# A two-block network in one launch: parked S5 matrices loaded pair by pair, small mixer weights split early, low parts of weights placed by clocks that know DVE and POOL exclude each other

## The chip, the cores and the metric

One core of a Trainium2 chip runs the whole program in one launch. The metric is the device time of one execution in microseconds; the kernel before takes 3071.73 us (median of three runs: 3071.64, 3071.73, 3073.94).

## The reference

Two blocks, one behind the other, on 256 tokens of 1024 numbers, all in float32. The first is a mixer of four kinds (differential attention, block attention, gated linear attention, a gated recurrence) and a mixture of 32 experts. The second has two layers, and each layer is three residual steps. The lines that matter here:

```python
for i in range(DEPTH_2):                                   # two layers
    f = swiglu(rmsnorm(h, ffn1_pre_g[i]), ...)             # 1024 -> 2 x 2816 -> 1024
    h = h + 0.5 * rmsnorm(f, ffn1_post_g[i])
    m = mixer(rmsnorm(h, mix_pre_g[i]), ...)
    h = h + rmsnorm(m, mix_post_g[i])
    f = swiglu(rmsnorm(h, ffn2_pre_g[i]), ...)
    h = h + 0.5 * rmsnorm(f, ffn2_post_g[i])
# the mixer of block 2
z, xbc, dt_raw, u5, g_a, g_b = split(u @ w_in)
y_a = ssd_branch(z, xbc, dt_raw, ...) @ w_branch_a         # state space, 4 groups of 8 heads, chunks of 128
y_b = s5_branch(u5, lam, b, c, ..., w_glu) @ w_branch_b    # complex diagonal recurrence, 64 groups
return (sigmoid(g_a) * y_a + sigmoid(g_b) * y_b) @ w_out
```

The S5 branch is computed in blocks of four tokens with matrices made from its parameters alone (powers of the eigenvalues times the input matrix, a Toeplitz matrix, an output matrix G, an array of powers E).

## The kernel before

**Weights.** A weight unit is 1 MB, a raw tile of 128 x 2048 float32, loaded by one DMA on SP into one of three raw buffers (`NRAW`). It has two halves of 128 x 1024. For each half ACT casts a high part (`whi`) and `tensor_sub` makes the low part (`wlo`, raw minus high) on DVE or on POOL; there are four pairs of high and low buffers. A half then feeds 24 matmuls of 128 x 256: three products (high x high, high x low, low x high) for each of eight slices. All of block 2's weights go this way: the two feed-forward steps of a layer (`ffn`), and in the mixer the stages u (input of S5), z, x and g (mixed in one plan, with the SSD's chunks between them), `glu` and `bb` (end of the S5 branch), `ba` (end of the SSD branch) and `wo`.

**What sets the order.** The order on every engine is fixed when the program is built, by a planner. `Clocks` and `Engine` keep an estimated clock for each engine (line 155 is the helper through which every instruction of block 2 and most of block 1 is issued; so the profile's lines are nearly all L155, and the work is told apart by the tiles' names). Side work is written as generators (threads): a thread issues a few instructions and yields; `yield n` with a whole number waits for ticks, with a float for that many microseconds of the planner's TensorE clock. `stir` steps, between groups of matmuls, those threads whose inputs would be ready by the clocks. `low(h)` chooses the engine of a low part: POOL, if POOL would be done in time for its matmuls or sooner than DVE, else DVE. `static` is the mode of the mixture of experts, whose order is written out by hand.

**Parked matrices.** Block 1 makes the S5 matrices while TensorE is waiting for expert weights and parks them in DRAM (`ld`, `kd`, `gd`, `ed`). `s5_build` is a thread that fetches them, in ffn1 of layer 0 and, for layer 1, in ffn2 of layer 0: for each half of the groups four loads of `ld` and four of the input matrix `s5_bt` (each 64 x 1024, 256 KB), eight small ones of `kd`, then a complex product (`cmul`, 12 instructions of 128 x 1024 on both halves), and last four loads of E and four of G (512 KB each). All go through SP's queue, where the weights are loaded too.

**Mixer.** `mixer` loads at its start the convolution's weights (`cw`) and the 1024 x 32 weight of dt (`dtw`), and scales and splits them in `small_weights` behind the third u unit; `ssd_steps` computes dt and its running sums from 32 rows (chain `dt`), transposes them on TensorE and hands over to four `ssd_group` threads, one for each group of heads. All four must have finished before `ba`.

Of the kernel before, what the change touches and what calls it, by code (L numbers as in the profile page):

```python
# [15 lines left out]
P = 128  # L16
# [26 lines left out]
class Clocks:  # L43
# [4 lines left out]
    def __init__(self, nc):  # L48
        self.nc, self.times, self.base = nc, {}, {}
        self.dma = self.queue = self.end = 0.0  # L50
        self.count, self.table = 0, None
        self.vector, self.gpsimd = Engine(nc.vector, self.on_vector, self), Engine(nc.gpsimd, self.on_gpsimd, self)
        self.scalar, self.tensor, self.sync = Engine(nc.scalar, self.on_scalar, self), Engine(nc.tensor, self.on_tensor, self), Engine(nc.sync, None, self)
# [52 lines left out]
    def busy(self, name):  # L106
        return max([max(t[:2]) for t in self.times.get(name, {}).values()], default=0.0)

    def on_vector(self, name, out, args, kw):
        n = max(a.free_size() for a in (out, *args) if isinstance(a, bass.AP))  # L110
        return 0.07 + 0.06 * any(isinstance(a, bass.AP) and a.free_size() == 1 for a in args) + n * (0.0063 if name == "reciprocal" else 0.00052 if name in self.SINGLE else 0.00104)
# [19 lines left out]
class Engine:  # L131
# [3 lines left out]
    def __getattr__(self, name):  # L135
        f, c = getattr(self.engine, name), self.clocks

        def call(out, *args, **kw):
            w = [out] + [kw[k] for k in ("accum_out",) if k in kw]
            r = [a for a in (*args, *kw.values()) if isinstance(a, bass.AP) and a is not kw.get("accum_out")]  # L140
            start = max([self.clock] + [c.written(a, self) for a in r] + [c.touched(a, self) for a in w])
            if name == "dma_start":
                self.clock = start + (1.0 if self is c.gpsimd else 0.1)
                c.queue = max(c.queue, start) + 0.45
                c.dma = max(c.dma, c.queue + 1.1) + self.spread(out, r)
                end = c.dma + 1.9
            else:
                end = self.clock = start + self.cost(name, out, args, kw)
            for a in w:
                c.mark(a, end, self)  # L150
            for a in r:
                c.mark(a, end)
            c.end = max(c.end, end)
            c.count += 1
            return f(out, *args, **kw)  # L155
        return call
# [22 lines left out]
class Core:  # L179
# [6 lines left out]
    NRAW = 3  # L186
    GAP = 20.0, 10.0, 25.0, 12.0
    LENT = ()
# [170 lines left out]
    def low(self, h):  # L359
# [4 lines left out]
        hi = c.written(self.halves[h][0])  # L364
        pool = max(self.q.clock, hi) + 2.3
        return self.q if pool <= max(c.tensor.clock + (h - self.uh) * 2.57 - self.LEAN, max(self.v.clock, hi) + 1.14) else self.v

# [74 lines left out]
    def step(self, th):  # L442
# [6 lines left out]
        if isinstance(th.wait, float):  # L449
            th.ready = c.tensor.clock + th.wait  # L450
        if th.done:
# [148 lines left out]
class Block2(Core):  # L600
# [406 lines left out]
    def s5_build(self, l, res):  # L1007
# [5 lines left out]
        self.lab = "s5b"  # L1013
        toep, win = [], []
        for hf in range(2):
            yield self.GAP[hf]
            yield from self.need(p4=8)
            self.lab = "s5b"
            tp = self.p4([P, H, 64])
            LT = self.p4([P, H, 64]), self.p4([P, H, 64])  # L1020
            BT = self.p4([P, H, 64]), self.p4([P, H, 64])
            for g in range(2):
                rows = slice(g * 64, g * 64 + 64)
                for ri in range(2):
                    nc.sync.dma_start(LT[ri][rows], dram_ap(ld, ((ri * 2 + g) * 4 * NP + hf * H) * 64, [[NP * 64, 4], [0, 16], [1, H * 64]]))
                    nc.sync.dma_start(BT[ri][rows], dram_ap(a["s5_bt"], (((l * 2 + ri) * 2 + g) * 16 * NP + hf * H) * 64,
                                                            [[0, 4], [NP * 64, 16], [1, H * 64]]))
                for j in range(4):
                    r0 = g * 64 + j * 16
                    nc.sync.dma_start(tp[r0:r0 + 16], dram_ap(kd, hf * H * 32 * 112 + g * 16 * 112 + (3 - j) * 16,  # L1030
                                                              [[112, 16], [32 * 112, H], [1, 64]]))
# [5 lines left out]
            self.give(p4=3 if hf else 5)  # L1037
            toep.append(tp)
            win.append((wr, wi))
        yield from self.need(p4=8)  # L1040
        self.lab = "s5b"
        G = [[self.p4([P, H, 4, 16]) for _ in range(2)] for _ in range(2)]
        E = [[self.p4([P, H, 64]) for _ in range(2)] for _ in range(2)]
        for hf in range(2):
            for ri in range(2):
                half = slice(ri * 1024, ri * 1024 + 1024)
                nc.sync.dma_start(E[hf][ri].rearrange("p h m -> p (h m)"), made["ed"][hf, :, half])
                nc.sync.dma_start(G[hf][ri].rearrange("p h k c -> p (h k c)"), made["gd"][hf, :, half])
            yield self.GAP[3]
        res.update(win=win, toep=toep, G=G, E=E, r4=made["r4"])  # L1050
# [143 lines left out]

    def ssd_steps(self, l, dps, r, res):

        nc, a, v = self.nc, self.a, self.v
        self.lab = "dt"
        hvt = self.t([32, 2], "hvt")
        nc.gpsimd.dma_start(hvt, a["hvec"][l])  # L1200
        y, e, u, w_, dt, adt, ac = (self.p1()[:32] for _ in range(7))
# [21 lines left out]
        for c in range(2):  # L1223
            cc = slice(c * P, c * P + P)
            v.tensor_tensor_scan(ac[:, cc], self.one32, adt[:, cc], 0.0, op0=ALU.mult, op1=ALU.add)
        yield 2
        yield from self.need(ps=1)
# [152 lines left out]


    def mixer(self, l, h, banks, build, s5):
        nc, a = self.nc, self.a
# [3 lines left out]
        self.lab = "u5"  # L1387
        cw = self.t([P, 24, 5], "cw")
        nc.sync.dma_start(cw, a["conv2"][l])
        dtw = self.p1([P, KD, 32])  # L1390
        nc.sync.dma_start(dtw, a["wdt"][l])
        dw = self.p1([P, KD, 32], F32R), self.p1([P, KD, 32], F32R)
        ud = self.scratch([1024, T], "ud")
# [37 lines left out]

        def small_weights():
            v.tensor_scalar_mul(cw, cw, 0.5)
            nc.scalar.copy(dw[0], dtw)
            yield
            v.tensor_sub(dw[1], dtw, dw[0].bitcast(F32))
# [14 lines left out]
        sd = {}  # L1451
        self.spawn(self.ssd_steps(l, dps, r, sd))
        self.finish(sc)
# [153 lines left out]
    def block2(self, h, layers=2, first=None):  # L1607
# [1389 lines left out]
```

## Time and profile before

| | us |
|---|---|
| median of three runs | 3071.73 |
| the profiled execution, its own time | 3076.65 |
| its span, first to last instruction | 3074.4 |
| TensorE busy | 2668.1 (87%) |
| DVE busy | 1689.6 (55%) |
| POOL busy | 1442.4 (47%) |
| ACT busy | 1020.0 (33%) |
| mean granted TensorE clock | 0.950 |

The profile is one execution. PE is TensorE, PEld its weight loads, SP the engine that issues most DMAs. "Busy" of DVE and POOL holds the time in which an instruction that has begun waits for the other of the two. Block 1's mixer runs to about 250 us, the experts from there to 1279 us; ffn1 of layer 0 lies at 1293 to 1517 us, its mixer at 1539 to 1966, ffn2 at 1986 to 2209; layer 1 follows in the same way to 3061 us.

### The profile page before, as it was taken

The numbers are of one execution on the slowest core, as the hardware profiler recorded it, in microseconds if no ns is written. First come the engines' busy times: TensorE is split into PE (matmuls) and PEld (weight loads), VectorE is DVE, ScalarE is ACT, GpSimd is POOL, SyncE is SP. The second block draws the span as 40 slices with busy tenths as digits, with TensorE's granted clock in tenths as the row PEclk, the third lists the DMA queues.
The fourth block names the chain that finished last, engine by engine and source line by source line (L and its number), as shares of the span: only waits on it lengthen the run. The fifth ranks groups of instructions, "written<-read, shape, count | busy, mean of one in ns | idle before, by whom it ended". The sixth has DMA issues, their size and how long they took to land.

```text
span 3074.4 us, 55096 instructions
## 1 busy us (share of the span) xinstructions
PE 2668.1 (87%) x22727; PEld 2062.3 (67%) x22727; DVE 1689.6 (55%) x2657; ACT 1020.0 (33%) x1516; POOL 1442.4 (47%) x733
## 2 busy tenths in 40 slices
PE   5768988889889888877989888977999889998998
PEld 4655333333333333577979888977999889888998
DVE  8995242333433211355577888655554685886644
ACT  4562100001000000233445554433444445544444
POOL 7651000000000000256756666756788657766786
PEclk9778999999999999998999999988999999999999
DMA  7526999999999999655545434455555445444453
GB/s 285 191 86 262 420 420 394 420 420 417 418 419 417 414 421 420 255 171 185 195 144 168 157 138 140 162 171 185 192 181 190 157 122 179 151 151 138 162 185 120
DMA packets 146540, 755.09 MB, mean 246 GB/s; under 512 B 47264, under 2 KB 51824, under 8 KB 59760
## 3 DMA queue, kind: packets, MB, share of 16 engines
q1 hardware_dynamic: 140672, 729.30, 62.6%
q0 software_dynamic: 5472, 21.71, 1.9%
q8 instruction: 183, 3.00, 0.4%
q14 instruction: 69, 0.57, 0.1%
q10 hardware_dynamic: 144, 0.52, 0.0%
HBM read 736.50 MB, written 14.97 MB: 244 GB/s over the span
## 4 chain that ended last, share of the span: by engine, by line
PE 36%; DVE 10%; issue 4%; DMA 3%; ACT 2%; POOL 2%; SPq 1%; ACTq 0%; DVEq 0%; POOLq 0%
PE ffn_ps L155 18%; PE x_ps L155 3%; PE ba_ps L155 3%; DVE ssd_p L155 3%; PE g_ps L155 2%; DMA s5b_p<-s_bt 2%; PE glu_ps L155 2%; PE bnd_ps L155 2%; PE z_ps L155 2%; POOL ffn_wlo L155 2%; PE wo_ps L155 1%; DVE x_p L155 1%; PE ssd_ps L155 1%; DVE u_p L155 1%; SPq L155 1%
## 5 line engine op out<-in xcount | busy, mean ns | idle before, releaser
L155 POOL TENSOR_TENSOR ffn_wlo<-ffn_raw,ffn_whi 128x1024 fp32r<-128x1024 f32 x227 | 569.9, 2537 | 178.4 <-ACT ffn_whi L155 172.7
L155 PE MATMUL ffn_ps<-bnd_p,ffn_whi 128*128 128x256 f32 x2560 | 469.2, 285 | 28.8 <-ACT ffn_whi L155 28.8
L155 PEld LDWEIGHTS ffn_ps<-bnd_p,ffn_whi 128*128 128x128 f32 x2560 | 404.5, 194 | 29.6 <-ACT ffn_whi L155 29.6
L155 PE MATMUL ffn_ps<-bnd_p,ffn_wlo 128*128 128x256 f32 x1280 | 366.4, 286 | 13.7 <-POOL ffn_wlo L155 13.7
L155 ACT CAST ffn_whi<-ffn_raw 128x1024 fp32r<-128x1024 f32 x232 | 240.3, 1046 | 259.4 <-PE ffn_ps L155 174.0
L155 PE MATMUL down_ps<-up_place,tr_p 128*32 128x512 f32 (+1 forms) x2048 | 244.0, 614 | 82.1 <-DMA up_place<-edn 82.1
L155 DVE TENSOR_TENSOR ffn_p<-ffn_p,ffn_p 128x256 f32<-128x256 f32 (+1 forms) x184 | 260.9, 1420 | 91.8 <-ACT ffn_p L155 91.4
L155 PE MATMUL ffn_ps<-ffn_p,ffn_whi 128*128 128x256 f32 x1408 | 258.9, 286 | 29.5 <-ACT ffn_whi L155 28.1
L155 PEld LDWEIGHTS ffn_ps<-bnd_p,ffn_wlo 128*128 128x128 f32 x1280 | 248.8, 194 | 15.9 <-POOL ffn_wlo L155 15.9
L155 PE MATMUL up_ps<-down_place,prep_p 128*32 128x512 f32 (+1 forms) x1920 | 224.8, 596 | 21.4 <-DMA down_place<-eup 21.3
L155 PEld LDWEIGHTS ffn_ps<-ffn_p,ffn_whi 128*128 128x128 f32 x1408 | 222.5, 194 | 30.1 <-ACT ffn_whi L155 28.5
L155 PE MATMUL up_ps<-up_place,prep_p 128*32 128x512 f32 (+1 forms) x2048 | 230.2, 595 | 8.3 <-DMA up_place<-eup 8.2
L155 PEld LDWEIGHTS down_ps<-up_place,tr_p 128*32 128x32 f32 x2048 | 67.8, 112 | 244.6 <-issue 200.5
L155 DVE TENSOR_SCALAR glu_p<-up_ps 128x512 f32<-128x512 f32 x64 | 44.1, 691 | 311.7 <-PE up_ps L155 311.7
L155 PE MATMUL ffn_ps<-ffn_p,ffn_wlo 128*128 128x256 f32 x704 | 201.0, 286 | 0.9 <-DVE ffn_wlo L155 0.9
L155 DVE TENSOR_TENSOR ffn_p<-ffn_ps,ffn_p 128x512 f32<-128x512 f32 x80 | 55.1, 689 | 208.6 <-PE ffn_ps L155 208.4
L155 PEld LDWEIGHTS up_ps<-up_place,prep_p 128*32 128x32 f32 x2048 | 61.8, 109 | 150.3 <-issue 129.1
L155 DVE COPY scat_p<-down_ps 128x512 f32<-128x512 f32 x16 | 11.1, 691 | 245.7 <-PE down_ps L155 245.7
L155 PEld LDWEIGHTS up_ps<-down_place,prep_p 128*32 128x32 f32 x1920 | 57.3, 109 | 129.2 <-issue 125.5
L155 PEld LDWEIGHTS ffn_ps<-ffn_p,ffn_wlo 128*128 128x128 f32 x704 | 136.7, 194 | 1.5 <-DVE ffn_wlo L155 1.5
L155 POOL DMA_DIRECT2D ed<-s5b_raw x4 | 2.1, 538 | 262.8 <-DVE s5b_raw L155 262.8
L155 POOL TENSOR_TENSOR scat_wlo<-scat_raw,scat_whi 128x1024 fp32r<-128x1024 f32 x2 | 4.7, 2364 | 251.1 <-ACT scat_whi L155 251.1
(832 smaller groups left out, 6547.7 us busy)
## 6 DMA issues: line engine op xcount, KB each, us to landing
up_place<-eup SPq DMA_DIRECT2D x128, 1024.0 KB, 10.9
up_place<-edn SPq DMA_DIRECT2D x128, 1024.0 KB, 13.7
down_place<-eup SPq DMA_DIRECT2D x120, 1024.0 KB, 14.1
ffn_raw<-gu SPq DMA_DIRECT2D x75, 1024.0 KB, 5.0
ffn_raw<-dn SPq DMA_DIRECT2D x40, 1024.0 KB, 4.9
x_raw<-win SPq DMA_DIRECT2D x22, 1024.0 KB, 5.0
z_raw<-win SPq DMA_DIRECT2D x16, 1024.0 KB, 4.9
g_raw<-win SPq DMA_DIRECT2D x10, 1024.0 KB, 5.4
```

The costliest lines, as they stand in the source:

```text
L155: return f(out, *args, **kw)
```

## The change

Five edits. (1) The planner's clocks keep for DVE and for POOL the stretches in which the other is at work; an instruction of one does not start inside one of the other, except a DVE instruction with an operand in PSUM. (2) `low` now takes DVE if DVE would be done in time or sooner than POOL. (3) A negative float after `yield` counts from the later of the planner's TensorE clock and the end of the thread's last work; the dt chain uses it ahead of its transposes. (4) `s5_build` issues its loads one or one pair at a time, with a pause behind each, and allots the Toeplitz and G tiles later. (5) `mixer_small`, a thread started ahead of ffn1, loads `cw`, `hvt` and `dtw` on SP and scales and splits them 40 us later; the mixer no longer does it.

```diff
@@ class Clocks
+    def shared(self, engine, start, time, ins):
+        other = self.port.get(self.gpsimd if engine is self.vector else self.vector, ())
+        if engine is self.vector and any(a.space == bass.MemoryType.PSUM for a in ins):
+            return start
+        for a, b in other:
+            if a <= start < b:
+                start = b
+        mine = self.port.setdefault(engine, [])
+        mine.append((start, start + time))
+        del mine[:-24]
+        return start
@@ class Engine, call
-                end = self.clock = start + self.cost(name, out, args, kw)
+                time = self.cost(name, out, args, kw)
+                if self is c.vector or self is c.gpsimd:
+                    start = c.shared(self, start, time, r)
+                end = self.clock = start + time
@@ low
-        pool = max(self.q.clock, hi) + 2.3
-        return self.q if pool <= max(c.tensor.clock + (h - self.uh) * 2.57 - self.LEAN, max(self.v.clock, hi) + 1.14) else self.v
+        pool, vec = max(self.q.clock, hi) + 2.3, max(self.v.clock, hi) + 1.14
+        return self.v if vec <= max(c.tensor.clock + (h - self.uh) * 2.57 - self.LEAN, pool) else self.q
@@ step
-            th.ready = c.tensor.clock + th.wait
+            th.ready = c.tensor.clock + th.wait if th.wait > 0 else max(c.end, c.tensor.clock) - th.wait
@@ s5_build
-    GAP = 20.0, 10.0, 25.0, 12.0
+    GAP = 8.0, 5.0, 8.0, 4.0
...
+        yield self.GAP[0]
         for hf in range(2):
-            yield self.GAP[hf]
-            yield from self.need(p4=8)
-            tp = self.p4([P, H, 64])
+            yield from self.need(p4=7)
             for g in range(2):
                 for ri in range(2):
                     nc.sync.dma_start(LT[ri][rows], ...)
                     nc.sync.dma_start(BT[ri][rows], ...)
-                for j in range(4):
-                    nc.sync.dma_start(tp[r0:r0 + 16], dram_ap(kd, ...))
+                    yield self.GAP[1]
             yield self.GAP[2]
...
+        for hf in range(2):
+            for ri in range(2):
+                nc.sync.dma_start(E[hf][ri]..., made["ed"][hf, :, ri * 1024:ri * 1024 + 1024])
+                yield self.GAP[1]
+        yield from self.need(p4=8)
+        toep = [self.p4([P, H, 64]) for _ in range(2)]
+        for hf in range(2):
+            for g in range(2):
+                for j in range(4):
+                    nc.sync.dma_start(toep[hf][r0:r0 + 16], dram_ap(kd, ...))
+                    yield self.GAP[3]
...
@@ ssd_steps
-        hvt = self.t([32, 2], "hvt")
-        nc.gpsimd.dma_start(hvt, a["hvec"][l])
...
-        yield 2
+        yield -6.0
@@ mixer, block2
+    def mixer_small(self, l):
+        ...
+        for t, w in ((cw, "conv2"), (hvt, "hvec"), (dtw, "wdt")):
+            nc.sync.dma_start(t, a[w][l])
+        self.small = cw, dw, hvt
+        yield 40.0
+        self.v.tensor_scalar_mul(cw, cw, 0.5)
+        nc.scalar.copy(dw[0], dtw)
+        yield
+        self.v.tensor_sub(dw[1], dtw, dw[0].bitcast(F32))
...
-            if g == 2:
-                sw = self.defer(small_weights)
-        self.finish(sw)
...
+            self.early = self.spawn(self.mixer_small(l))
             acc = self.ffn(l, h, banks, g, vec("f1pre"))
```

Since the planner sets the order, the edits move instructions on all engines. Three places are shown; the line of the helper is 155 before and 172 after.

On SP, in ffn1 of layer 0, before (`ffn_raw` are weight loads, `s5b_p` the S5 tiles):

```order
L155 DMA ffn_raw_9324<-gu 128x2048
L155 DMA s5b_p_1328_9333<-ld_3203 64x1x1024
L155 DMA s5b_p_1330_9335<-s_bt 64x1x1024
L155 DMA s5b_p_1329_9334<-ld_3203 64x1x1024
L155 DMA s5b_p_1331_9336<-s_bt 64x1x1024
L155 DMA s5b_p_1327_9332<-kd_3944 16x16x64 x4
...
L155 DMA ffn_raw_9409<-dn 128x2048
```

The same place after the change:

```order
L172 DMA ffn_raw_9148<-gu 128x2048
L172 DMA s5b_p_1312_9198<-ld_3213 64x1x1024
L172 DMA s5b_p_1314_9200<-s_bt 64x1x1024
L172 DMA ffn_raw_9221<-dn 128x2048
L172 DMA s5b_p_1313_9199<-ld_3213 64x1x1024
L172 DMA s5b_p_1315_9201<-s_bt 64x1x1024
L172 DMA ffn_raw_9286<-gu 128x2048
```

Before, 16 S5 loads stand between two weight loads (the cut leaves out a second set of eight); after, one pair stands between two weight loads, and the `kd` loads come later in the same ffn.

On DVE, in ffn2 of layer 0, before (`ffn_p` are the activation's steps, one of them from PSUM); the low parts of this stretch stand on POOL:

```order
L155 TENSOR_TENSOR ffn_p_2321_16938<-ffn_ps_16867,ffn_p_2215_16229 128x512
L155 TENSOR_TENSOR ffn_p_2322_16939<-ffn_p_2322_16939,ffn_p_2321_16938 128x256
L155 TENSOR_TENSOR ffn_p_2325_16953<-ffn_p_2322_16939,ffn_p_2324_16952 128x256
L155 TENSOR_TENSOR ffn_p_2330_17005<-ffn_ps_16928,ffn_p_2215_16229 128x512
L155 TENSOR_TENSOR ffn_p_2331_17006<-ffn_p_2331_17006,ffn_p_2330_17005 128x256
```

On DVE in the same ffn2 of layer 0, after the change:

```order
L172 TENSOR_TENSOR ffn_wlo_17386<-ffn_raw_17218,ffn_whi_17385 128x1024
L172 TENSOR_TENSOR ffn_p_2390_17422<-ffn_ps_17344,ffn_p_2215_16239 128x512
L172 TENSOR_TENSOR ffn_p_2391_17423<-ffn_p_2391_17423,ffn_p_2390_17422 128x256
L172 TENSOR_TENSOR ffn_wlo_17414<-ffn_raw_17218,ffn_whi_17413 128x1024
L172 TENSOR_TENSOR ffn_p_2394_17437<-ffn_p_2391_17423,ffn_p_2393_17436 128x256
L172 TENSOR_TENSOR ffn_wlo_17454<-ffn_raw_17303,ffn_whi_17453 128x1024
```

The low parts now stand in DVE's queue between the activation's steps. Counted from block 2's first weight on, 22 of the 488 low parts of weights stand on DVE before and 471 after; the other 17 stay on POOL.

On PE, from the end of `bb` to the first `ba` of layer 0, before (`ssd_ps` are matmuls of the SSD groups, `bb_ps` and `ba_ps` weight matmuls):

```order
L155 MATMUL bb_ps_15045<-glu_p_2004_14544,bb_wlo_14970 128x256
L155 MATMUL ssd_ps_15119<-ssd_p_2069_15002,ssd_p_2067_14989 128x512
L155 MATMUL bb_ps_15122<-glu_p_1945_14172,bb_whi_15012 128x256
...
L155 MATMUL ssd_ps_15147<-ssd_p_2070_15004,ssd_p_2084_15145 64x128
...
L155 MATMUL bb_ps_15122<-glu_p_2004_14544,bb_whi_15012 128x256
...
L155 MATMUL ssd_ps_15178<-ssd_p_2070_15004,ssd_p_2084_15145 64x128
...
L155 MATMUL bb_ps_15122<-glu_p_2004_14544,bb_wlo_15047 128x256
L155 MATMUL ssd_ps_15230<-ssd_p_2092_15207,k_ones_g_95 128x256
L155 MATMUL ba_ps_15253<-ssd_p_1950_14185,bb_whi_15082 128x256
```

The same place after the change (`k_ident` marks transposes, `k_ones_g` a group's mean):

```order
L172 MATMUL bb_ps_15002<-glu_p_1979_14444,bb_wlo_14935 128x256
L172 MATMUL ssd_ps_15082<-k_ident_87,x_p_1769_12553 128x128
L172 MATMUL ssd_ps_15086<-k_ident_87,x_p_1890_13738 128x128 x4
L172 MATMUL ssd_ps_15087<-k_ident_87,x_p_1890_13738 128x128 x4
L172 MATMUL ssd_ps_15098<-ssd_p_2031_14793,ssd_p_2044_14874 64x128
...
L172 MATMUL ssd_ps_15149<-ssd_p_2077_15144,k_ones_g_95 128x256
L172 MATMUL ssd_ps_15190<-ssd_p_2079_15151,ssd_p_2074_15135 128x512
L172 MATMUL ssd_ps_15198<-ssd_p_2063_15078,ssd_p_2075_15137 64x128
...
L172 MATMUL ssd_ps_15241<-ssd_p_2092_15237,k_ones_g_95 128x256
L172 MATMUL ba_ps_15263<-ssd_p_1946_14174,bb_whi_14973 128x256
```

Before, the last group's 24 products stand between `bb` matmuls, 30 of which follow, and only its mean stands behind the last of them. After, 62 matmuls of the SSD stand between the last `bb` matmul and the first `ba`: the third group's 24 products and mean, and the last group's transposes, state product, 24 products and mean.

## Rows read from the trace of the kernel before

**Rows 1.** Page, part 1: busy time of each engine.

```profile
PE 2668.1 (87%) x22727; PEld 2062.3 (67%) x22727; DVE 1689.6 (55%) x2657; ACT 1020.0 (33%) x1516; POOL 1442.4 (47%) x733
```

**Rows 2.** Windows by stage: length, busy PE, PEld, DVE, ACT, POOL, clock, DMA share, GB/s.

```profile
250.00:1278.90 1028.90, 892.18 (x7728) 341.11 (x7726) 313.30 (x919) 85.77 (x148) 38.30 (x44) 0.98 0.99 408
1293.50:1516.80 223.30, 186.25 (x1491) 184.06 (x1489) 118.08 (x89) 84.61 (x116) 153.32 (x62) 0.92 0.56 189
...
1628.00:1781.80 153.80, 142.47 (x1424) 138.49 (x1423) 116.50 (x164) 83.94 (x114) 108.35 (x50) 0.97 0.49 165
1781.80:1857.00 75.20, 63.02 (x504) 59.20 (x503) 62.58 (x93) 38.23 (x54) 50.30 (x23) 0.93 0.40 140
1857.00:1896.00 39.00, 31.60 (x256) 29.78 (x255) 33.11 (x49) 15.85 (x20) 23.04 (x11) 0.91 0.41 137
...
1986.20:2209.00 222.80, 186.26 (x1490) 184.05 (x1488) 119.04 (x88) 83.01 (x113) 154.21 (x62) 0.92 0.56 190
2230.70:2410.00 179.30, 178.75 (x1490) 178.55 (x1488) 86.26 (x74) 83.69 (x113) 154.55 (x65) 1.00 0.53 183
```

**Rows 3.** Waits of PE in ffn1 of layer 0: total, times, longest.

```profile
PE ffn_ps L155 <- ACT ffn_whi L155: 28.2, 3, 14.4
PE ffn_ps L155 <- POOL ffn_wlo L155: 6.3, 4, 1.9
```

**Rows 4.** Waits of ACT in the same stretch.

```profile
ACT ffn_whi L155 <- DMA ffn_raw<-gu: 20.5, 3, 17.9
```

**Rows 5.** Chain of waits, 1300 to 1440 us: start, length, what.

```profile
1322.49 16.04 DMA s5b_p<-s_bt
...
1340.61 4.16 SPq L155
...
1344.89 9.65 DMA ffn_raw<-dn
```

**Rows 6.** Windows inside and behind that stall, columns as in rows 2.

```profile
1342.00:1347.00 5.00, 0.00 (x0) 0.00 (x0) 0.00 (x0) 0.00 (x0) 0.00 (x0) 0.91 0.31 105
1352.00:1355.00 3.00, 0.00 (x0) 0.00 (x0) 0.00 (x0) 0.36 (x1) 0.00 (x0) 0.50 1.00 418
...
1358.00:1361.00 3.00, 3.00 (x21) 3.00 (x20) 2.52 (x3) 1.56 (x3) 3.00 (x2) 0.70 0.33 63
```

**Rows 7.** DMA issues: queue, count, KB each, median us to landing.

```profile
ffn_raw<-gu SPq DMA_DIRECT2D x75, 1024.0 KB, 5.0
...
ssd_p<-acd POOLq DMA_DIRECT2D x16, 512.0 KB, 5.8
...
s5b_p<-kd SPq DMA_DIRECT2D x32, 64.0 KB, 12.7
```

**Rows 8.** Waits of PE from u to ba of layer 0.

```profile
PE ssd_ps L155 <- DVE ssd_p L155: 13.1, 7, 5.1
PE dt_ps L155 <- DVE dt_p L155: 7.9, 2, 4.2
...
PE u_ps L155 <- DVE u_p L155: 4.7, 1, 4.7
...
PE u_ps L155 <- ACT u_p L155: 1.6, 1, 1.6
```

**Rows 9.** Low parts and activation steps: count, ns min/median/max, first and last start.

```profile
L155 POOL TENSOR_TENSOR ffn_wlo<-ffn_raw,ffn_whi x59: 2397/2418/2651, 2229.1 to 2406.0; 128x1024 fp32r<-128x1024 f32 x59
...
L155 DVE TENSOR_TENSOR glu_wlo<-glu_raw,glu_whi x2: 1210/1210/1210, 1830.3 to 2723.5; 128x1024 fp32r<-128x1024 f32 x2
...
L155 DVE TENSOR_TENSOR ffn_p<-ffn_p,ffn_p x46: 411/1471/2694, 2235.7 to 2409.6; 128x256 f32<-128x256 f32 x24, 128x256 fp32r<-128x256 f32 x22
```

**Rows 10.** Chain of waits, 1857 to 1902 us, from bb to ba.

```profile
1857.82 1.43 PE ssd_ps L155 x13
...
1883.52 7.80 issue
...
1896.72 5.41 PE ba_ps L155 x44
```

More of the change, by code (lines that the diff above doesn't have):

```diff
@@ L51, in __init__ @@
         self.count, self.table = 0, None
+        self.port = {}
         self.vector, self.gpsimd = Engine(nc.vector, self.on_vector, self), Engine(nc.gpsimd, self.on_gpsimd, self)
@@ L1014, in s5_build @@
         toep, win = [], []
+        yield self.GAP[0]
         for hf in range(2):
-            yield self.GAP[hf]
-            yield from self.need(p4=8)
-            self.lab = "s5b"
-            tp = self.p4([P, H, 64])
+            yield from self.need(p4=7)
             LT = self.p4([P, H, 64]), self.p4([P, H, 64])
@@ L1024, in s5_build @@
                 for ri in range(2):
+                    self.lab = "s5b"
                     nc.sync.dma_start(LT[ri][rows], dram_ap(ld, ((ri * 2 + g) * 4 * NP + hf * H) * 64, [[NP * 64, 4], [0, 16], [1, H * 64]]))
@@ L1027, in s5_build @@
                                                             [[0, 4], [NP * 64, 16], [1, H * 64]]))
-                for j in range(4):
-                    r0 = g * 64 + j * 16
-                    nc.sync.dma_start(tp[r0:r0 + 16], dram_ap(kd, hf * H * 32 * 112 + g * 16 * 112 + (3 - j) * 16,
-                                                              [[112, 16], [32 * 112, H], [1, 64]]))
+                    yield self.GAP[1]
             yield self.GAP[2]
@@ L1036, in s5_build @@
                 yield
-            self.give(p4=3 if hf else 5)
-            toep.append(tp)
+            self.give(p4=5)
             win.append((wr, wi))
-        yield from self.need(p4=8)
+        yield from self.need(p4=4)
         self.lab = "s5b"
-        G = [[self.p4([P, H, 4, 16]) for _ in range(2)] for _ in range(2)]
         E = [[self.p4([P, H, 64]) for _ in range(2)] for _ in range(2)]
@@ L1045, in s5_build @@
             for ri in range(2):
[L1046 to L1049, printed above, removed]
+                self.lab = "s5b"
+                nc.sync.dma_start(E[hf][ri].rearrange("p h m -> p (h m)"), made["ed"][hf, :, ri * 1024:ri * 1024 + 1024])
+                yield self.GAP[1]
+        yield from self.need(p4=8)
+        self.lab = "s5b"
+        toep = [self.p4([P, H, 64]) for _ in range(2)]
+        for hf in range(2):
+            for g in range(2):
+                for j in range(4):
+                    self.lab = "s5b"
+                    r0 = g * 64 + j * 16
+                    nc.sync.dma_start(toep[hf][r0:r0 + 16], dram_ap(kd, hf * H * 32 * 112 + g * 16 * 112 + (3 - j) * 16,
+                                                                    [[112, 16], [32 * 112, H], [1, 64]]))
+                    yield self.GAP[3]
+        self.lab = "s5b"
+        G = [[self.p4([P, H, 4, 16]) for _ in range(2)] for _ in range(2)]
+        for hf in range(2):
+            for ri in range(2):
+                self.lab = "s5b"
+                nc.sync.dma_start(G[hf][ri].rearrange("p h k c -> p (h k c)"), made["gd"][hf, :, ri * 1024:ri * 1024 + 1024])
+                yield self.GAP[1]
         res.update(win=win, toep=toep, G=G, E=E, r4=made["r4"])
@@ L1191, in s5_run, with ssd_steps @@
         self.give(p4=2)
-    def ssd_steps(self, l, dps, r, res):
+    def ssd_steps(self, hvt, dps, r, res):
         nc, a, v = self.nc, self.a, self.v
         self.lab = "dt"
-        hvt = self.t([32, 2], "hvt")
-        nc.gpsimd.dma_start(hvt, a["hvec"][l])
         y, e, u, w_, dt, adt, ac = (self.p1()[:32] for _ in range(7))
@@ L1378, in ssd_group @@
         self.give(p4=1)
+    def mixer_small(self, l):
+        nc, a = self.nc, self.a
+        self.lab = "msm"
+        cw, hvt, dtw = self.t([P, 24, 5], "cw"), self.t([32, 2], "hvt"), self.t([P, KD, 32], "dtw")
+        dw = self.t([P, KD, 32], "dwh", dt=F32R), self.t([P, KD, 32], "dwl", dt=F32R)
+        for t, w in ((cw, "conv2"), (hvt, "hvec"), (dtw, "wdt")):
+            nc.sync.dma_start(t, a[w][l])
+        self.small = cw, dw, hvt
+        yield 40.0
+        self.lab = "msm"
+        self.v.tensor_scalar_mul(cw, cw, 0.5)
+        nc.scalar.copy(dw[0], dtw)
+        yield
+        self.v.tensor_sub(dw[1], dtw, dw[0].bitcast(F32))
     def mixer(self, l, h, banks, build, s5):
@@ L1387, in mixer @@
         self.lab = "u5"
[L1388 to L1392, printed above, removed]
+        self.finish(self.early)
+        cw, dw, hvt = self.small
         ud = self.scratch([1024, T], "ud")
@@ L1430, in mixer @@
         self.budget = self.BM
[L1432 to L1436, printed above, removed]
         for g in (2, 3):
@@ L1451, in mixer @@
         sd = {}
-        self.spawn(self.ssd_steps(l, dps, r, sd))
+        self.spawn(self.ssd_steps(hvt, dps, r, sd))
         self.finish(sc)
```

## The prediction

> **What bounds the kernel now.** The page's busy times come first [rows 1]: TensorE is at work for 87% of the span, DVE for 55%, POOL for 47%. An average over unlike stages decides nothing, so the second view is the table by stage [rows 2]. It shows three kinds. The experts (250 to 1279 us) use 0.99 of the DMA engines: DMA sets their 1029 us, and their order is written out by hand. The ffn without S5 loads (ffn1 of layer 1) is TensorE from end to end, 178.75 of 179.30 us at clock 1.00, and ffn2 of layer 1 reads alike. The two ffns with S5 loads (ffn1 and ffn2 of layer 0) take 223.3 and 222.8 us for the same matmuls (1491 and 1490 against 1490): 44.0 and 43.5 us more. Last, the mixer's stages leave TensorE idle in pieces: 11.3 us in g and x (153.8 - 142.5), 12.2 in glu, 7.4 in bb.
>
> Where the 44 us come from is read from three further views. PE waits 28.2 us for high parts and 6.3 for low parts [rows 3]; its busy time is 7.5 us longer (186.25 - 178.75), since the granted clock is low behind a stall: 0.50 at its end, still 0.70 three microseconds after work resumed [rows 6]. 28.2 + 6.3 + 7.5 = 42.0. ACT, which makes the high parts, waits in turn for the weight's DMA, 17.9 us at the longest [rows 4]. The chain says why [rows 5]: from 1322.49 us the S5 loads fill the queue, kd holds SP for another 4.16 us at the end, and the next weight load is issued at 1344.89 and lands 9.65 us later, at 1354.54: 32.1 us without a new weight. A half is 24 matmuls, so 1490 of them are 62 halves and a half takes 178.75 / 62 = 2.88 us; three raw buffers hold six halves, 17.3 us. 32.1 - 17.3 = 14.8, and the longest wait is 14.4 us. The buffers thus cover 17 us of a gap, no more.
>
> **Spread loads.** The same loads are issued, but the two bursts become pairs with a weight load between. A pair is 512 KB; inside the burst 105 GB/s moved [rows 6], so it takes 4.9 us. With two issues of about half a microsecond each and even the slow landing of 9.65 us, a weight comes 4.9 + 1.1 + 9.65 = 15.7 us behind its forerunner's issue, inside the 17.3 us. E and G go at the weights' own rate (512 KB at 418 GB/s: 1.2 us). A kd load is 64 KB, but lands only after 12.7 us [rows 7] and held SP for 4.16; one between two weights is inside the cover too (4.2 + 9.65 = 13.9). So the stalls go, with them the slow clock behind them. Late next is nothing but the low parts: the 6.3 us of POOL's go, but 12 complex products now on POOL (2.4 us each [rows 9], 29 us) hold DVE up, which has low parts to make; I leave 2.7 us for that and take 182 us for each of the two ffns, 223.3 - 182 = 41 us less, 82 for both. Ends: 44 (all of the difference), and 30 (one of three stalls, 14.4 us, stays, for instance at kd).
>
> [...]
>
> **Low parts to DVE.** From block 2's first weights on, 471 of 488 stand on DVE instead of 22 (449 move). One takes 1.21 us there against 2.42 on POOL [rows 9]. In ffn1 of layer 1 that is 62 x 1.21 = 75 us on DVE, beside its own steps: 20 from PSUM and 46 of 128 x 256, whose shortest takes 0.41 and whose median 1.47 us, because POOL's low parts hold them up [rows 9]. Unheld, those 46 are 19 us, the 20 from PSUM 14 (0.69 us each); with the rest DVE has some 113 us of work in 179, so an ffn of layer 1 is unchanged (within 1 us): TensorE has no gap to give back there.
>
> **Mixer, for each layer.** Small weights: PE waits in u 4.7 us for DVE and 1.6 for ACT [rows 8], for that split; it now stands in ffn1, where 4 halves of cover hide it. I take -6; ends 0 (the last u step waits for something else) and -6.3. The dt transposes wait 7.9 us [rows 8]; after, they are placed 6 us behind their chain's planned end, with other matmuls in front; I take -7, ends -3 and -7.9. In g, x and glu PE waits mostly for ssd_p and x_p on DVE (13.1 us over the mixer, [rows 8]), where 0.42- to 0.68-us steps are stretched to 2.4 to 2.8 by POOL's low parts. With these gone the steps are short, but DVE has more to do in all: about 117 us of 154 in g and x. I take 11.3 to 5 and 12.2 to 5.5, -13 together; ends +3 and -18.
>
> The end of bb goes the other way. Before, the last group's transposes run at 1857.82 us and ba begins at 1896.72 [rows 10]: a chain of 38.9 us, of which bb's matmuls filled nearly all, 7.4 us idle [rows 2]. After, by the order, that group's transposes come behind bb's last matmul, and ba waits for the whole group. The chain loses stretches in which its steps stood behind others (7.8 us "issue" [rows 10], and steps of 2.5 us that POOL held up): I take 33 us. 13 SSD matmuls took 1.43 us [rows 10], so the 62 in it work for about 8 us, which leaves 25 us idle against 7.4: +18. Ends: +8 (DVE far quicker than before) and +31 (the full 38.9 stays: 38.9 - 8 = 31 idle, +24, and 7 for a queue of ba's low parts ahead of the chain's steps). The slow clock behind stalls costs 11 us in a mixer now by the same reckoning as in the ffn (three stalls, 7.5); fewer short stalls give back 3, one long one takes some: I take -2, ends 0 and -5. Sum for a layer: -6 - 7 - 13 + 18 - 2 = -10, ends -29 and +21; for both -20.
>
> [...]
>
> **Block 1 and the experts.** The mixer of block 1 moves about 23 low parts from POOL to DVE, where DVE is the busier engine already; I take 0, ends -8 and +10. Experts 0.
>
> **Sum.** The profiled execution took 3076.65 us; -82 - 20 = -102 gives 2975. It ran 4.9 us over the median of three runs (3071.73), and the forecast is for the median: **2970 us**. Own range, with stages adding up unlike: 2940 to 3000. What a measurement can tell from no change is 0.2%, some 6 us.
>
> **Rivals.** (a) The mixer loses: DVE, now the only maker of low parts, delays the chains, g, x and glu stay as they are (-13 gone), and the end of bb is at its upper end (+31): a layer -6 - 7 + 31 - 2 = +16, both +32, so 3072 - 82 + 32 = 3022. For it: the order puts two groups' work behind bb in layer 0; against it: DVE's steps lose POOL's stretching. (b) The spread doesn't do what it says: weights still come late since four engines stay loaded through most of the ffn (4 MB at 105 GB/s, 40 us in each), half of the stalls stay: 3072 - 41 - 20 = 3011; with all of them 3052. Against it: the 17.3 us of cover. (c) Slower: DVE works in order, so a low part stands behind steps that wait for PE's sums or ACT, while PE waits for that low part. POOL, with only low parts in an ffn, never waited so. The place is each half of each weight stage, the price up to 1.21 us a half. 488 halves at 0.21 us eat the 102 us; that is the point from which it decides. With every second half late by a whole low part: 244 x 1.21 = 295, so 2970 + 295 = 3265. Against it: DVE idles 66 us in an ffn by the sum above, and the four buffer pairs let a low part be made up to 11 us early. (d) Better: the end of bb costs no more than +8 and all other terms are at their ends: 3072 - 88 - 2 x 29 = 2926.
>
> **Chances.** Forecast 0.58; (a) 0.16; (b) 0.11; (c) 0.06; (d) 0.09. The range that holds 8 in 10 takes the forecast, (a) and most of (d): 2926 to 3030. Faster by over 0.2%: all but (c) and the worst of (a) and (b), 0.91; within 0.2%: 0.03; slower: 0.06.
>
> **What will show it.** Right: both ffns of layer 0 at 180 to 186 us with a clock near 1.00 and no wait for high parts over 3 us; no wait in u for the split; the dt wait under 3 us; one new wait of PE of 15 us or more at the end of bb, for DVE or ACT on ssd_p. Wrong: waits of some 14 us for high parts in ffn1 (then b); many waits of about 1 us for low parts on DVE in all weight stages (then c); no stall at the end of bb (then the order's tail is cheaper than the chain before).

## The result, and the profile after

The changed kernel takes 2963.64 us (median of four runs, 2959.05 to 2967.87) against 3072.74: ratio 0.9645, 95% interval [0.9626, 0.9663]. The profiled execution took 2960.17 us, its span is 2958.4 us, its mean clock 0.965 (0.950 before). The two profiled executions lie 116.5 us apart, the medians 109.1: the one before ran 3.9 us over its median, this one 3.5 under.

By stage (lengths from the two traces, us; the first line is the start of block 2):

| | before | after | forecast of the change | measured |
|---|---|---|---|---|
| end of block 1 | 1278.9 | 1291.5 | 0 | +12.6 |
| ffn1, ffn2 of layer 0 | 223.3, 222.8 | 198.0, 197.8 | -41 each | -25 each |
| ffn1, ffn2 of layer 1 | 179.3, 179.7 | 178.7, 178.7 | 0 | -1 |
| mixer of layer 0, u to wo | 427.0 | 388.5 | -10 | -38.5 |
| ... u | 22.8 | 14.5 | -6 | -8.3 |
| ... z (holds the dt chain) | 66.2 | 55.5 | -7 | -10.7 |
| ... g and x | 153.8 | 138.2 | -6 | -15.6 |
| ... glu | 75.2 | 54.2 | -7 | -21.0 |
| ... bb until ba begins | 39.0 | 56.5 | +18 | +17.5 |

The mixer's terms of the forecast (but for -2 for the clock) are idle time of PE, the measured column is lengths, in which moved matmuls count too. Idle time alone changed by -6.3 in u, -7.9 in z, -10.2 in g and x, -11.0 in glu and +11.7 in bb.

Layer 1's mixer shows the same. The table by stage of the changed kernel (columns as in rows 2; against the same stages there, and u, z in the third and fourth line):

```profile
250.00:1291.50 1041.50, 906.45 (x7844) 355.65 (x7843) 322.99 (x952) 94.80 (x166) 38.45 (x50) 0.98 0.98 404
1306.00:1504.00 198.00, 184.20 (x1490) 181.95 (x1488) 120.44 (x139) 85.11 (x115) 35.64 (x14) 0.98 0.63 202
...
1526.00:1540.50 14.50, 14.50 (x125) 14.35 (x124) 14.33 (x27) 6.18 (x10) 0.00 (x0) 1.00 0.92 320
1540.50:1596.00 55.50, 55.50 (x615) 53.92 (x614) 49.47 (x84) 30.37 (x40) 4.59 (x7) 1.00 0.58 185
1596.00:1734.20 138.20, 137.06 (x1443) 133.94 (x1442) 123.06 (x191) 79.22 (x108) 37.94 (x25) 1.00 0.56 190
1734.20:1788.40 54.20, 52.96 (x452) 51.65 (x451) 42.98 (x74) 32.88 (x47) 9.83 (x8) 1.00 0.48 160
1788.40:1844.90 56.50, 37.40 (x321) 34.22 (x320) 43.99 (x89) 24.52 (x30) 14.83 (x13) 0.85 0.31 109
```

Before, u and z, which rows 2 leaves out:

```profile
1539.00:1561.80 22.80, 16.50 (x123) 15.24 (x122) 20.09 (x29) 8.05 (x15) 15.71 (x7) 0.85 0.56 185
1561.80:1628.00 66.20, 58.32 (x645) 56.34 (x644) 50.90 (x76) 26.67 (x33) 34.60 (x22) 0.95 0.44 129
```

From u to glu TensorE now works with 2.4 us of idle time in all, at clock 1.00; idle time and low clock are gone together. Nearly all that this mixer still loses lies in the last line: 19.1 us idle at clock 0.85.

Waits of PE in ffn1 of layer 0 (against rows 3), and the chain of waits there (start, length, what; against rows 5):

```profile
PE ffn_ps L172 <- DVE ffn_wlo L172: 8.6, 7, 2.7
PE ffn_ps L172 <- ACT ffn_whi L172: 5.1, 3, 3.3
```

```profile
1320.00 16.44 DMA ffn_raw<-gu
...
1372.46 14.37 DMA ffn_raw<-gu
...
1390.40 16.68 DMA ffn_raw<-gu
```

The waits of 14 us are gone, but these weights, and a fourth issued at 1341.56, landed only 14 to 17 us after their issue (5.0 us is the median before, rows 7). A window in this stretch shows why; the columns are those of rows 2:

```profile
1356.00:1358.00 2.00, 0.24 (x2) 0.24 (x3) 2.00 (x2) 1.57 (x3) 1.92 (x2) 1.00 0.24 102
```

0.24 of the DMA engines carry 102 GB/s while PE starves, as in the burst before (0.31 and 105, rows 6): the S5 pairs hold about a quarter of the 16 engines.

DVE's steps in ffn1 of layer 1, which were 411/1471/2694 ns [rows 9]:

```profile
L172 DVE TENSOR_TENSOR ffn_p<-ffn_p,ffn_p x46: 415/420/426, 2159.4 to 2333.3; 128x256 f32<-128x256 f32 x24, 128x256 fp32r<-128x256 f32 x22
```

None is held up any more, and 57 low parts beside them take 1.22 us each. The 20 steps with an operand in PSUM took 677/691/693 ns before, with POOL at work for 154.55 of the stretch's 179.30 us [rows 2], and 680/692/694 after: those were not held up.

### The profile page after: what moved, and what is told of

Same layout as the page of the kernel before. It is cut to its first block, busy times and chain, and to the rows that moved or that the text cites. A ratio compares the mean times of both kernels' runs of the same rounds, so it can differ in the third digit from the quotient of the medians.

```text
span 2958.4 us, 54963 instructions
## 1 busy us (share of the span) xinstructions
PE 2631.0 (89%) x22727; PEld 2033.5 (69%) x22727; DVE 1727.5 (58%) x3032; ACT 1037.3 (35%) x1534; POOL 442.5 (15%) x346
## 4 chain that ended last, share of the span: by engine, by line
PE 45%; DVE 5%; DMA 4%; ACT 2%; issue 1%; POOL 0%; ACTq 0%; DVEq 0%; SPq 0%
PE ffn_ps L172 18%; PE x_ps L172 5%; DMA ffn_raw<-gu 4%; PE z_ps L172 3%; PE ba_ps L172 3%; PE g_ps L172 3%; PE glu_ps L172 3%; PE bnd_ps L172 2%; PE wo_ps L172 2%; PE bb_ps L172 2%; PE ssd_ps L172 1%; DVE ffn_wlo L172 1%; DVE bnd_p L172 1%; PE u_ps L172 1%; PE s5o_ps L172 1%; DVE ssd_p L172 1%
## 5 line engine op out<-in xcount | busy, mean ns | idle before, releaser
L172 DVE TENSOR_TENSOR ffn_wlo<-ffn_raw,ffn_whi 128x1024 fp32r<-128x1024 f32 x232 | 300.9, 1301 | 203.0 <-ACT ffn_whi L172 202.9
L172 ACT COPY prep_p<-prep_ps 128x512 f32<-128x512 f32 x16 | 9.4, 585 | 288.5 <-PE prep_ps L172 288.5
L172 DVE TENSOR_TENSOR ffn_p<-ffn_p,ffn_p 128x256 f32<-128x256 f32 (+1 forms) x184 | 85.2, 468 | 41.7 <-ACT ffn_p L172 41.4
L172 ACT COPY tr_p<-tr_ps 128x512 f32<-128x512 f32 x32 | 18.7, 586 | 222.3 <-PE tr_ps L172 222.3
L172 ACT ACTIVATE glu_p<-glu_p 128x512 f32<-128x512 f32 (+1 forms) x48 | 26.8, 558 | 187.5 <-DVE glu_p L172 187.5
```

## The experiments

**1. The spread alone** (on the kernel before, `s5_build` and `GAP` as in the change).

> The kernel before with the new fetching of the parked S5 matrices alone (pairs, pauses, later tiles), everything else as before. Theory 1 (the parts add up): the two ffns of layer 0 fall from 223 us to about 198 us each, as in the whole change, and block 1 and the mixers stay as before: 3072 - 50 = 3022 us. Rival (the ffns' gain needs the low parts on DVE too, since POOL with 2.42 us for each half of 2.88 us cannot catch up once a weight is late): the ffns fall to only 207 to 212 us, 3040 to 3050 us in all.

Measured: 3030.47 us, ratio 0.9862 [0.9845, 0.9878]. The ffns take 198.5 and 204.5 us, mixers and block 1 are within about 3 us of before. The time lies between the two theories; alone, the spread is worth 42 us.

**2. All but the spread** (the changed kernel with the old `s5_build` and `GAP`).

> The whole change but with the old fetching of the S5 matrices (two bursts of 16 loads). Theory 1: the two ffns are back at about 223 us each, mixers and block 1 as after the change: 2964 + 50 = 3014 us. Rival (DVE, quicker at low parts, takes part of the stalls away by itself): ffns at 210 to 215 us, 2985 to 2998 us in all. Waits of PE for high parts of about 14 us, three in each of these ffns, by both.

Measured: 2982.68 us, ratio 0.9708 [0.9691, 0.9724]; the rival holds. The two stalls left in ffn1 show it (waits of PE):

```profile
PE ffn_ps L172 <- ACT ffn_whi L172: 18.8, 2, 10.0
```

The longest is 10.0 instead of 14.4 us: with the bursts unchanged, the ffns fall to 210 and 207 us. In the whole change the spread is worth 19 us (2983 to 2964), not 42 and not the 82 of the forecast.

**3. The rule and the clocks alone** (on the kernel before).

> The kernel before with the clocks' exclusion and the new rule for low parts alone; S5 loads, small weights and the dt chain as before. Theory 1: block 1 is longer by 12 to 13 us as after the change, the ffns of layer 0 lose only POOL's 6 us, and each mixer gains what is left of its 38.6 us without the u and dt stages' part (8.4 + about 8): 3072 + 12.6 - 12 - 2 x 22 = 3029 us. Rival (the mixers' gain is mostly the small weights and the dt chain, the low parts give little): mixers within 8 us of before, 3060 to 3075 us in all.

Measured: 2986.92 us, ratio 0.9733 [0.9716, 0.9749], below both theories. The mixers take 393.0 and 393.2 us, and u takes 14.2 us though the small weights are split where they were:

```profile
1531.20:1545.40 14.20, 14.20 (x122) 14.05 (x121) 14.03 (x28) 6.31 (x10) 0.00 (x0) 1.00 0.82 285
```

POOL is idle in u (0.00 against 15.71 us busy before), so the wait for the split was most likely for DVE's steps behind POOL's low parts; before, one of u's steps took 2578 ns where the median is 412. z takes 55.6 us, as after the whole change, with a dt wait of 0.7 us, though the dt chain stands as before.

**4. S5 loads over more engines** (the changed kernel; the same bytes in transfers of 16 rows).

```diff
-nc.sync.dma_start(LT[ri][rows], dram_ap(ld, ..., [[NP * 64, 4], [0, 16], [1, H * 64]]))
-nc.sync.dma_start(BT[ri][rows], dram_ap(a["s5_bt"], ..., [[0, 4], [NP * 64, 16], [1, H * 64]]))
+for j in range(4):
+    r16 = slice(g * 64 + j * 16, g * 64 + j * 16 + 16)
+    nc.sync.dma_start(LT[ri][r16], dram_ap(ld, ..., [[0, 16], [1, H * 64]]))
+    nc.sync.dma_start(BT[ri][r16], dram_ap(a["s5_bt"], ..., [[NP * 64, 16], [1, H * 64]]))
```

> The changed kernel, with each S5 load of 64 x 1024 cut into four of 16 x 1024 whose outermost dimension is 16, so the same bytes in four times as many transfers. Theory 2 (what is left in the ffns of layer 0, 198 against 179 us, is a backlog on the few engines that carry the S5 loads: a pair takes 4.9 us there and the weight's share 2.5, together 7.4 us for each 5.8 us of work): the transfers go over all engines, a pair takes about 1.3 us, both ffns fall to 180 to 185 us and the time to about 2934 us. Rival (the rest is DVE held up by POOL's complex products and SP's issuing): the ffns stay at 195 us or more, or get longer by SP's 48 more issues of about half a microsecond; 2955 to 2975 us.

Measured: 2940.55 us, ratio 0.9571 [0.9555, 0.9587]; theory 2 holds, but for its time of a pair. ffn1 of layer 0 (ffn2 takes 179.0 us), columns as in rows 2:

```profile
1310.60:1490.70 180.10, 179.22 (x1491) 178.64 (x1489) 124.72 (x139) 85.65 (x116) 36.47 (x14) 1.00 0.68 222
```

The stall is gone though SP issues four times as many transfers and POOL, with the complex products, is as busy as after the change (36.5 us against 35.6), so neither part of the rival is the cause. A stretch of that ffn with S5 loads and no weight in flight:

```profile
1369.00:1372.00 3.00, 3.00 (x27) 3.00 (x26) 1.96 (x4) 1.91 (x4) 0.00 (x0) 1.00 0.63 122
```

More than four of the 16 engines carry them: 0.63 against 0.31 in the burst before [rows 6] and 0.24 after the change, with an outermost dimension of 16 where it was four. The rate hardly rose (122 GB/s against 105), so a pair of 512 KB takes 4.3 us, not the 1.3 expected. SP took 0.54 us in the median to issue one of the S5 loads of the changed kernel; if one of 64 KB takes as long, that is 121 GB/s (an estimate), which may be what limits it. What fell is the load on each engine: 0.63 x 4.3 = 2.7 us for a pair, with the weight's 2.5 some 5.2 us, under the 5.8 of work, where it was 7.4 on four engines (an estimate from these rows). Weights land after 5.1 us again (median of the run's 75 `gu` loads).

The gain is 37 us in the ffns and 23 in all, since in layer 0 g and x grew from 138 to 151 us, 8.7 of them a wait of PE for a low part on DVE: the S5 stage was planned later and fell into x.

**5. Block 1 by the old plan** (the changed kernel; `low` and `shared` as before until the experts).

> The changed kernel, but block 1's mixer planned by the old clocks and the old rule for low parts (its order is then the one before, instruction for instruction, up to the experts). Theory 3 (the new plan of block 1's mixer costs its 12.6 us: the output projection starts at 256 instead of 240 us): block 1 ends at 1278 to 1281 us again, all else as after, 2950 us. Rival (the longer block 1 is the experts' DMA-bound part, or its scatter from run to run): block 1 ends at 1288 us or later, 2957 to 2968 us.

Measured: 2950.29 us, ratio 0.9612 [0.9596, 0.9628]; block 1 ends at 1277.0 us. Theory 3 holds. With the new plan, block 1's mixer has this wait of PE, which before has not:

```profile
PE ab_ps L172 <- ACT gla_p L172: 17.8, 1, 17.8
```

Others are shorter (PE's `gla_ps` waits for DVE fell from 21.2 to 4.1 us), so which of them costs the 13 us was not followed. In the traces of all runs, the seven with the old plan of block 1 end it at 1275 to 1279 us, and the seven with the new rule, the new clocks or both at 1289 to 1297.

**6. SSD groups start earlier** (the changed kernel).

```diff
-    SPARE = 2
+    SPARE = 0
```

> The changed kernel with one number changed: an SSD group may start with four free pages instead of six (SPARE 0). By the order, the fourth group's transposes then come in the middle of bb and only 26 matmuls of the SSD instead of 62 stand between the last bb matmul and the first ba. Theory 4 (the 31 to 33 us without weight matmuls ahead of ba are the last group's chain, exposed because it starts one group late): that stretch falls to 8 to 15 us, glu and bb grow by what the moved matmuls take (about 5 us), so each mixer gains 12 to 18 us, 2964 - 30 = 2934 us. Rival (the chain's DVE steps only wait elsewhere: the groups run side by side and hold each other up on DVE, and glu and bb get the waits): mixers within 5 us of after, 2955 to 2970 us.

Measured: 2955.97 us, ratio 0.9628 [0.9612, 0.9645]; the mixers are 1 and 4 us shorter, as the rival has it. The 7.7 us in all are not clear of the noise: the interval overlaps that of the changed kernel. Theory 4 falls: fewer matmuls stand behind bb, yet bb until ba still takes 53.2 us (56.5 after the change).

```profile
1792.00:1845.20 53.20, 37.99 (x311) 34.43 (x310) 45.75 (x86) 23.67 (x30) 14.06 (x12) 0.87 0.32 113
```

Counted from bb's start, the chain through DVE and ACT ends only 3.3 us earlier, though its matmuls moved. DVE is at work for 45.8 of the 53.2 us (44.0 of 56.5 after the change), which fits the rival: groups that run side by side take turns on DVE.

**7. Early small weights and later dt transposes alone** (on the kernel before).

> The kernel before with the early small weights and the later dt transposes alone; low parts still on POOL by the old rule. Theory 5 (the split of the small weights was late because DVE's steps stand behind POOL's low parts, and it costs nothing any more once the low parts are on DVE, since with the rule and the clocks alone u took 14.4 us too): alone on the kernel before it still takes the wait of 6 us out of u and most of the 8 us out of dt, 3072 - 2 x 10 = 3052 us; in the whole change it is worth only the 4 us a layer by which the mixer is shorter than with the rule alone. Rival (the terms of my forecast: both are worth their full waits in either kernel): u 16 us and the dt wait under 1 us, 3072 - 2 x 14 = 3044 us or less. Third: other waits take their place, 3066 us or more.

Measured: 3061.45 us, ratio 0.9969 [0.9957, 0.9982]: between theory 5 and its third case. u falls to 14.2 us and the dt wait to 1.7, but z grows from 66.2 to 79.7. 9.7 us of that are PE's own work (838 matmuls instead of 645; g and x and glu are 4 and 5 us shorter), and PE there has a new wait:

```profile
PE z_ps L155 <- POOL z_wlo L155: 7.9, 2, 6.7
```

With POOL as the maker of low parts, new waits take up part of what the two edits remove; the mixers as wholes are 4 and 7 us shorter.

**8. Experiments 4, 5 and 6 together.**

> The changed kernel with S5 loads over sixteen engines, block 1's old plan, and SSD groups starting with four free pages. If the three gains add up (23 us measured for the first; 13 and 30 expected for the others): 2964 - 23 - 13 - 30 = 2898 us. If the earlier groups give nothing: 2925 to 2930 us.

Measured: 2916.92 us, ratio 0.9502 [0.9486, 0.9518]. The three measured gains (23.1, 13.4 and 7.7) give 2919.5: they add up, though the third is not clear of the noise by itself.

**9. The rule alone** (on the kernel before).

> The kernel before with the new rule for low parts alone (DVE first); the planner's clocks don't know the exclusion. Theory 6 (the rule does the work, since nearly all low parts leave POOL by it: 460 of 488 on DVE by the order, and with POOL empty there is little exclusion left to know): within 10 us of the rule and the clocks together, 2977 to 2997 us. Rival (without the exclusion the planner puts steps where POOL holds DVE up, and its order is late in the mixers): 3005 us or more.

Measured: 2986.20 us, ratio 0.9732 [0.9715, 0.9749], the same as with the clocks (0.9733). Theory 6 holds. The rule gives 85 us by itself, where the whole change gives 109. The mixers take 388.1 and 391.4 us, as after the whole change (388.4 and 390.2), so on top of the rule the other edits give the mixers next to nothing. Block 1 ends at 1290.2 us. The ffns of layer 0 take 207.9 and 209.0 us though the S5 loads come in the old bursts; ffn1:

```profile
1304.40:1512.50 208.10, 185.51 (x1490) 183.62 (x1488) 120.43 (x137) 84.93 (x114) 34.22 (x14) 0.93 0.57 203
```

PE waits there twice for high parts, 18.7 us in all, instead of three times and 28.2 [rows 3]. How quicker low parts shorten the stalls was not followed.

**10. The clocks alone** (on the kernel before).

> The kernel before with the clocks' exclusion alone; the old rule keeps 421 of 488 low parts on POOL. Theory 6: the steps of DVE stay stretched by POOL's low parts, a plan that knows it can only move work, 3050 to 3085 us. Rival (knowing the exclusion is what makes the mixers shorter): mixers 15 us or more shorter each, 3040 us or less.

Measured: 3032.76 us, ratio 0.9870 [0.9853, 0.9887]: the rival's size, and here theory 6 falls. With 421 low parts still on POOL, the planner by these clocks finds an order whose ffns take 208.7 and 207.0 us and whose mixers are 9.5 and 13.5 us shorter, while block 1 is 11 us longer, as with the rule alone. Alone, the clocks are thus worth 38 us. Why each stage moved was not followed further. It does not add to the rule.

**11. Early halves of ba** (experiment 8's kernel; the first halves of the first three ba units, which need groups 0 and 1 only, ahead of the wait for the others).

```diff
+self.finish(*groups[:2])
+early, kept = [self.bank() for _ in range(3)], []
+for n in range(5):
+    w = self.half(("ba", n // 2), max(n, 1))
+    if n % 2:
+        kept.append(w)
+    else:
+        ba_half(w, 0, early[n // 2])
 self.finish(*groups)
```

> The kernel with sixteen engines, block 1's old plan and four free pages (2917 us), and the first halves of the first three ba units, which need the SSD groups 0 and 1 only, moved ahead of the wait for groups 2 and 3: 72 matmuls, 8.6 us of TensorE, now stand between the last bb matmul and the last group's work. Theory 7 (the last group's chain of DVE and ACT steps sets the start of the rest of ba, whatever TensorE does meanwhile, so work that doesn't need it is hidden there): each mixer 7 to 9 us shorter, 2900 to 2903 us. Rival (the ba halves need low parts from DVE, which hold the chain up by the same time: 5 x 1.2 us): 2909 to 2917 us.

Measured: 2913.53 us, ratio 0.9482 [0.9466, 0.9498], against experiment 8's [0.9486, 0.9518]: the intervals overlap. bb and ba together take 97.8 us in layer 0 instead of 101.0 in experiment 8, and 97.6 instead of 102.3 in layer 1. So 3.2 and 4.7 us of the 8.6 are gained: between theory 7 and the rival. The chain of waits from the last group's mean to ba, here and in experiment 8 (start, length, what):

```profile
1825.87 1.21 PE ssd_ps L172 x2
...
1831.31 4.70 PE ba_ps L172 x22
```

```profile
1820.62 1.19 PE ssd_ps L172 x2
1821.81 2.19 PE ba_ps L172 x11
```

The rest of ba begins 59.9 us behind bb's start (1771.4), 5.9 us later than ba does in experiment 8 (54.0 behind 1767.8). The mean itself comes only 1.7 us later (54.5 against 52.8 us behind bb's start). Two more low parts are made ahead of it, one on DVE (1.22 us) and one on POOL (2.41), not the five that the rival counts. The other 4.2 us lie behind the mean. In experiment 8 ba begins at once, with first halves that don't need the last group, and they hide ACT's and DVE's last steps on that group. Here those halves are used up, and ba goes on 5.4 us behind the mean's start instead of 1.2. Part of the 8.6 us of work had thus hidden the chain's tail already.

**12. The same with shorter pauses** (`GAP` 6, 3, 6, 2.5).

> The kernel of the run before with shorter pauses in the S5 loads (6, 3, 6 and 2.5 us instead of 8, 5, 8 and 4). With all engines carrying them the weights have room: ffns stay at 179 to 181 us, and in layer 0 the S5 stage no longer falls into x, where DVE was late by 8.7 us: its g and x stretch falls from 153 to 138 us as in layer 1, 12 to 15 us less than the run before, 2886 to 2891 us. Rival (the denser loads make weights late again, or the x stage has another cause): 2895 us or more.

Measured: 2917.82 us, ratio 0.9506 [0.9490, 0.9522]. Theory and rival each came in part: g and x of layer 0 fall to 137.2 us, and the ffns of layer 0 grow, ffn2 to 189.3 us and ffn1 to 185.3:

```profile
1293.00:1478.30 185.30, 181.26 (x1490) 180.25 (x1488) 129.46 (x136) 85.20 (x115) 45.59 (x17) 0.99 0.70 228
```

By the medians the gain is given back. The quickest versions are those of experiments 8, 11 and 12, which the intervals don't tell apart, 5% under the kernel before.

## Why the prediction was right, and where it was not

The time, 2970 us forecast and 2963.64 measured, and its sign came out, but that the sum came so close was luck. Large terms were wrong in opposite directions: the ffns fell short by 32 us, block 1 cost 12.6, and the two mixers gave 58 us more than forecast. The shares are turned round, too. The forecast has 82 of its 102 us from the spread, which on top of the other edits is worth 19 (experiment 2). For the low parts it counts 13 us a mixer and a few us in each ffn of layer 0; the rule alone is worth 85 (experiment 9).

Of the signs, the waits in u for the split and in z for dt are gone. The ffns of layer 0 took 198 us, not 180 to 186, and their longest wait for high parts was 3.3 us. The end of bb shows waits of 19.1 us, but the longest single one is 7.3 us, and for a step on POOL, not one of 15 for DVE or ACT.

**Spread loads: the step that failed** is "a weight comes 15.7 us behind its forerunner's issue, inside the 17.3 us". It counted one pair. Four pairs follow each other. With no weight in flight the S5 loads kept a quarter of the 16 engines busy, four (0.25 and 96 GB/s from 1342 to 1344 us of the trace before), and weights all of them (1.00 and 418 GB/s [rows 6]). So I estimate from these shares that a weight puts a quarter of its bytes on the four engines that the pairs hold: 256 KB, half a pair, 2.5 us. With the pair's 4.9 that is 7.4 us for every 5.8 us of TensorE's work, so by this estimate the four engines fall 1.6 us further behind with each unit. It gives a backlog that grows, not its size: landing took 14 to 17 us. Experiment 4 speaks for the engines as the cause: with the same bytes at a share of 0.63, these ffns took 180.1 and 179.0 us. The delay of one transfer was in the sum, the load over several was not. Of the 19.3 us that ffn1 keeps (198.0 against 178.7), 13.7 are waits for high and low parts and 5.5 are PE's longer busy time at clock 0.98. Rival (b) had named the cause, four engines that stay loaded, with half of the stalls left; the ffns kept 18 to 19 of their 44 us, and experiments 2 and 9 add that part of what went was the rule's doing.

**Low parts: right in kind, mis-sized in the mixers.** No gap opened in the ffns of layer 1 (178.7 us). In the mixer the steps lost their stretching as forecast, but the forecast left 5 us of waits in g and x, and about as much in glu; 1.1 and 1.2 us stayed. Its reading of the waits was loose: of the 13.1 us for ssd_p on DVE, 7.4 lie in bb and ba; in g, x and glu it is 5.7, with 6.3 for x_p. The clock term was mis-sized most: from u to bb PE's busy time fell by 14.5 us (311.9 to 297.4) for the same work (2952 and 2956 matmuls), not by 2, with the clock from 0.97 to 1.00 in g and x. With idle time down by 23.6 us, not 8, that is the mixer's 38 us. In glu, 52 matmuls also moved on into bb (504 to 452), so glu and bb together say more than each: 114.2 to 110.7.

**Small weights and dt: right in place, wrong in cause.** Both waits are gone (-8.3 and -10.7 in length). But the rule alone removes u's wait and leaves 1.6 us of dt's (experiment 9), and the two edits alone are worth 9 us in 3071 (experiment 7). On top of the rule and the clocks they leave the mixers 4 us shorter a layer (393 against 389 in experiment 2), which the rule without the clocks reaches too.

**End of bb: right in kind, its size partly by luck.** The forecast's +18 is idle time, 25 us against 7.4. Measured, it is 19.1 us, so +11.7; the stretch is 17.5 us longer because 5.8 us more of PE's work stand in it too (321 matmuls instead of 256). The chain behind bb was put at 33 us with 25 idle and 8 of PE's work. It has 30.9, with 19.1 idle and 11.8 of work (the trace shows 113 PE instructions where the order has 62 matmuls), and DVE is busy for most of it:

```profile
1813.70:1844.60 30.90, 11.82 (x113) 9.12 (x112) 23.70 (x54) 11.65 (x15) 8.24 (x9) 0.72 0.17 62
```

Experiments 6 and 11 speak for the chain, and not the place of its matmuls, as what sets this length: moving the matmuls gained 3.3 us of 56.5, and filling the idle time with 8.6 us of other work 3.2. No run made the chain itself shorter, so it is argued, not shown.

The upper end of a layer's range is mis-added: the upper ends as listed give 0 - 3 + 3 + 31 + 0 = +31, not +21. The acd loads, POOL's own, landed hardly later with the low parts on DVE: after 6.1 us in the median (5.8 before) and 9.0 at the longest (7.6).

**Block 1: wrong**, outside its own ends (-8 to +10). I looked at which engine makes the low parts, and counted them wrong: by the trace 7 moved to DVE (20 of 30 instead of 13), not 23. Experiment 5 shows that the new plan is what cost, and the rule alone and the clocks alone each cost 11 us there (experiments 9 and 10); which step of the plan does it stays open. Rivals (a), (c) and (d) did not come: the mixers gained, PE's waits for low parts on DVE are 8.6 us in ffn1 of layer 0 and none in ffn1 of layer 1, and the end of bb cost more than 8.

## What to carry to other kernels

A load that uses few DMA engines (a share of 0.24 to 0.31 of the 16 here) has to be weighed by the time it takes on those engines, together with the share of all other traffic on them, over every period and not once; here giving its outermost dimension sixteen took 37 us out of the ffns on top of the spread, which took 22 on top of the other edits. Sixteen without the spread was not run. Where the long pieces of one engine hold up another's steps, as POOL's low parts of 2.42 us did DVE's here, move them to the engine that does them in short ones (1.22 us on DVE), even if that engine is the busier: the steps beside them get shorter (420 instead of 1471 ns in the median here). A planner's edit changes all that it plans, so look at the stages it was not meant for, and undo it there.

## What was not expected of the hardware

Nothing beyond sizes: DVE at 0.89 of a stage (g and x, 123.06 of 138.20 us) let TensorE run there with 1.1 us of waits, and 32 loads of 256 KB that sat on a quarter of the DMA engines (shares of 0.24 to 0.31) could be cut into 128 of 64 KB with 37 us less in the ffns, the issues hidden. That the cut loads moved hardly more bytes a second (122 GB/s against 105) on twice the share of engines (0.63 against 0.31) was not foreseen either; that SP's issuing limits them fits the numbers and was not tested.
